# A hybrid decoder trunk on one core: for every fourth weight unit the high part comes by a GpSimd DMA instead of a ScalarE copy

## The chip, the core and the metric

The kernel runs on one core of a Trainium2 chip. What counts is the device time of one execution in microseconds (us), the median over runs. Before the change it is 2649.82 us (3 runs, 2649.51 to 2650.46).

The core has five engines that run side by side: TensorE (PE in the profile; its weight loads are PEld), VectorE (DVE), ScalarE (ACT), GpSimd (POOL) and SyncE (SP, which here only issues DMAs).

## The reference

A trunk of two layers over 256 tokens of 2048 features, in float32. Layer 0 mixes tokens by retention (8 heads), layer 1 by sliding-window attention (32 query heads, 4 key/value heads). Each layer then has a SwiGLU network of hidden width 5632 and a gated embedding.

```python
for i in range(DEPTH):
    h = rmsnorm(x, norm_mix[i])
    if i % N_MIXERS == 0:
        x = x + retention_mixer(h, ret_w_in[j], ret_gn[j], ret_w_out[j])
    else:
        x = x + swa_mixer(h, swa_w_in[j], swa_sinks[j], swa_w_out[j])
    x = x + swiglu(rmsnorm(x, norm_ffn[i]), ffn_w_in[i], ffn_w_out[i])
    gate = jax.nn.sigmoid(rmsnorm(x, norm_ple[i]) @ ple_w_gate[i])
    x = x + gate * (p[i] @ ple_w_proj[i])
return rmsnorm(x, norm_final)
```

Nearly all of the work is in the products of activations with weights. The weights, about 0.49 GB, are read from memory once.

## The kernel before

**Split products.** A float32 product is made of float32r parts: an activation and a weight are each split into a high part (hi, the value rounded to float32r) and a low part (lo, the value less hi). Each product is three matmuls: hi by hi, lo weight by hi activation, hi weight by lo activation (lines 159 to 161).

**Units and chunks.** A chunk is 512 output columns for all 256 tokens, summed up in two PSUM tiles. It is made of units: 256 rows of a weight by 512 columns, 512 KB that lie in memory in one piece, 4 KB for each of 128 partitions. A unit gives 2 row blocks x 2 token tiles x 3 = 12 matmuls of 512 columns. There are 928 units in one list over six stages: retention (units 0 to 255; a head's q and k, v, and g are 8 units each), network 0 (to 519), embedding 0 (to 555), attention (to 627), network 1 (to 891), embedding 1 (to 927).

**Buffers and order.** `run` walks the list. In step i it loads unit i + LOADS (5) into a raw buffer by one SP DMA (`load`), splits unit i + AHEAD (3) in `split_weights` (ACT copies raw to hi on line 208, DVE subtracts on line 209), and multiplies unit i. Behind a chunk's last unit its `done` takes the sums out of PSUM. Then comes one step of the side work: pieces of the heads' own work, transposes by DVE (line 233, four for each step), and the splits of the next activation. There are 5 raw, 4 hi and 4 lo buffers of 4 KB a partition. A raw buffer is free when the unit's subtraction is done, a hi or lo buffer when the unit's matmuls are done.

Each engine works off its instructions in a fixed order. This order comes from a planner that goes by the order of the code, but lets an instruction that it holds to be ready go ahead of one that is not.

**The start.** The first norm's activation (xT) comes transposed from memory in eight pieces, which pass through the raw buffers too (`load_x`, line 744): the first three between the loads of units 0, 1 and 2, the others in the side work of steps 0 to 4. ACT and DVE put a piece in place (lines 211 and 212). In the same steps x itself is loaded in four pieces.

**GpSimd** does little: two fills at the start, and 24 powers (`pow`) of a few columns, of which the retention's rs (line 360) come two for each head, after DVE's statistics of a head's output.

Of the kernel before, what the change touches and what calls it, by code (L numbers as in the profile page):

```python
# [18 lines left out]
P = 128  # L19
D = 2048  # L20
S = 256
# [17 lines left out]
STEP = 4  # L39
LOADS = 5  # L40
AHEAD = 3


class Lhs:
    """A transposed activation, split exactly into two float32r parts."""

# [8 lines left out]
class Chunk:  # L55
    """512 output columns for all tokens, accumulated over the whole contraction, in pieces of
    a token tile and some of the columns."""

# [6 lines left out]
class Unit:  # L65
    """KU blocks of 128 rows of a weight, in one chunk's columns."""

    def __init__(self, chunk, src, kts, lhs):
        self.chunk, self.src, self.kts, self.lhs = chunk, src, kts, lhs
        self.w = None  # L70


class Stage:
    """A part of the trunk with tiles of its own, from its first unit to its last."""

# [3 lines left out]
    def linear(self, w, block, lhs, done, units=None, chunk=None):  # L79
        """One chunk: block of 512 columns of a weight laid out by `_units`."""  # L80
        ch = chunk or Chunk(self, done)
        for u in units if units is not None else range(w.shape[1]):
            self.units.append(Unit(ch, w[block, u], range(KU * u, KU * u + KU), lhs))
            ch.left += 1
# [3 lines left out]
def tile_trunk(ctx, tc, ins, out):  # L88
    nc = tc.nc
    pool = ctx.enter_context(tc.tile_pool(name="persist", bufs=1))  # L90
    wraw = ctx.enter_context(tc.tile_pool(name="wraw", bufs=5))
    whi = ctx.enter_context(tc.tile_pool(name="whi", bufs=4))
    wlo = ctx.enter_context(tc.tile_pool(name="wlo", bufs=4))
# [13 lines left out]

    # ---------------------------------------------------------------- streams
    side = deque()
# [15 lines left out]
    def load(u, pieces=1):  # L125
        raw = wraw.tile([P, KU, NW], F32, name="raw")
        n = KU // pieces
        u.parts = [slice(j, j + n) for j in range(0, KU, n)]
        for part in u.parts:
            nc.sync.dma_start(raw[:, part, :], u.src[:, part, :])  # L130
        u.w = raw

    def split_weights(u):
        raw = u.w
        hi = whi.tile([P, KU, NW], F32R, name="hi")
        lo = wlo.tile([P, KU, NW], F32R, name="lo")
        for part in u.parts:
            split(hi[:, part, :], lo[:, part, :], raw[:, part, :])
        u.w = (hi, lo)

    def multiply(u, which, left):
        """The unit's products for some pieces of its chunk; `left` of the chunk's units are
        still to come."""
        ch = u.chunk
        need(u.lhs, u.kts)
        if ch.acc is None:
            ch.acc = []
            for n, (_, cols) in enumerate(ch.pieces):
                bank, name = (ps_acc, "acc") if n < NT else (ps_at, "at")
                ch.acc.append(bank.tile([P, NW], F32, name=name)[:, : cols.stop - cols.start])  # L150
        hi, lo = u.w
        for j, k in enumerate(u.kts):
            first = not ch.begun and j == 0
            last = left == 0 and j == KU - 1
            for n in which:
                t, cols = ch.pieces[n]
                sl = slice(t * P, (t + 1) * P)
                xh, xl = u.lhs.hi[:, k, sl], u.lhs.lo[:, k, sl]
                nc.tensor.matmul(ch.acc[n], xh, hi[:, j, cols], start=first, stop=False)  # L159
                nc.tensor.matmul(ch.acc[n], xh, lo[:, j, cols], start=False, stop=False)  # L160
                nc.tensor.matmul(ch.acc[n], xl, hi[:, j, cols], start=False, stop=last)  # L161

    def run(stages, begin):
        """All units in order, their weights AHEAD units ahead; between them, steps of side work.
        The products of the units that end the last chunk go piece by piece of its output."""
        units = [(st, u) for st in stages for u in st.units]
        for n, (_, u) in enumerate(units[:LOADS]):
            if n < AHEAD:
                next(begin)
            load(u, 1 if n else KU)  # L170
            if n < AHEAD:
                split_weights(u)
# [31 lines left out]

    # ------------------------------------------------------------ small pieces
    def split(hi, lo, src, scale=None):
# [9 lines left out]
    def transpose_pair(srcs):  # L216
        """Two [128, 128] blocks of both token tiles -> a PSUM tile [128, 2, S]."""
        tr = ps_tr.tile([P, 2, S], F32, name="tr")
        for j, pair in enumerate(srcs):
            for t in range(NT):  # L220
                nc.tensor.transpose(tr[:, j, t * P : (t + 1) * P], pair[t], ident)
        return tr

    def transposes(dst, src):
        """Steps that transpose src [128, NT, 512] into dst [128, 4, S], by blocks of 32 x 32."""
        n = P // SQ
# [10 lines left out]
    def blocks(src, i):  # L237
        """Blocks 2i and 2i + 1 of 128 columns of both token tiles."""
        return [[src(t)[:, b * P : (b + 1) * P] for t in range(NT)] for b in (2 * i, 2 * i + 1)]

    class Norm:
        """Sums of squares of the residual's chunks, and the transposed residual times the gain.
        The scale by token, inv, is applied behind the product with the weights."""

# [22 lines left out]
        def places(self, c, src):  # L267
            """Steps that put a chunk's four transposed blocks in place."""
            for j in range(4):
                if j % 2 == 0:  # L270
                    yield
                self.place(4 * c + j, src[:, j, :])
# [5 lines left out]
    def residual(stage, norm, c):  # L278
        """A chunk of an output projection onto the residual, then the next norm's part."""

# [14 lines left out]

    # --------------------------------------------------------------- retention
    def retention(norm, next_norm, w_in, w_out):
# [97 lines left out]

    # ---------------------------------------------------- sliding-window attention
    def swa(norm, next_norm, w_in, w_out):
# [36 lines left out]
        def q_done_of(j):  # L434
            def q_done(acc):
# [12 lines left out]
                def scores(i):  # L448
                    """Of heads 2i and 2i + 1: the numerators and denominators' parts."""
                    ats = [ps_at.tile([P, 3 * P], F32, name="at") for _ in range(2)]  # L450
# [97 lines left out]
        for j in range(SKV):  # L548
            stage.linear(w_in, j, norm.lhs, q_done_of(j))
        # The first chunks' last units wait for the last group of heads.  # L550
        n = KD // KU
# [7 lines left out]

    # --------------------------------------------------------------------- FFN  # L560
    def ffn(layer, norm, next_norm):
# [57 lines left out]

    # --------------------------------------------------------------------- PLE  # L620
    def ple(layer, norm, next_norm, final):
# [12 lines left out]
        def pair(c):  # L634
# [3 lines left out]
            def gate_done(acc):  # L638
# [7 lines left out]
                def later():  # L646
                    # The last reads of the old operand are queued: its place is free.
                    for b, xt in enumerate(st["xt"]):
                        yield from next_norm.places(b, xt)
# [34 lines left out]
            def gate_last(acc, t, cols):  # L684
                """A piece of the last chunk; with a token tile's last one, its rows go out."""
                fin, rest, row = st["fin"], st["rest"], xs[:, t, :]
# [37 lines left out]

    # ------------------------------------------------------------------- trunk
    norms = [Norm(w, layer) for layer in range(DEPTH) for w in range(3)] + [Norm(None, 0)]
# [14 lines left out]
    def load_x():  # L741
        """The first norm's operand comes transposed, in step with the first chunk's weights."""
        for b in range(KD // KU):
# [19 lines left out]
def _constants():  # L763
    """Tables that follow from the shapes alone."""
    h = np.arange(RH, dtype=np.float64)
# [14 lines left out]
def _units(w):  # L780
    """[K, N] -> [N / 512, K / 256, 128, 2, 512]: each unit in one piece, by partitions."""
    k, n = w.shape
    return w.reshape(k // (KU * P), KU, P, n // NW, NW).transpose(3, 0, 2, 1, 4)


def _heads(w):
    """The retention's columns by heads: q and k, v, g."""
    q, k, v, g = np.split(w, [RH * RK, 2 * RH * RK, 2 * RH * RK + RH * RV], axis=1)
    parts = [a.reshape(D, RH, -1) for a in (q, k, v, g)]
    return np.concatenate(parts, axis=2).reshape(D, -1)  # L790
# [44 lines left out]
```

## Time and profile before

| what | value |
|---|---|
| median of the runs | 2649.82 us |
| span of the profiled execution, first to last instruction | 2647.9 us |
| its granted TensorE clock, mean | 0.999 |
| PE busy | 2629.2 us, 99% |
| DVE busy | 1817.2 us, 69% |
| ACT busy | 1223.7 us, 46% |
| POOL busy | 14.6 us, 1% |
| read from memory | 493.63 MB, 187 GB/s over the span |

The profiled execution's own time is its span and what lies around it. The record holds the span alone; the median of the runs is 1.9 us above it. Busy time of PE is modelled for pipelined matmuls, so that it is not a measure of how near PE is to its peak.

### The profile page before, as it was taken

What the parts mean: (1) busy time and instruction counts of PE and PEld (TensorE: products, weight loads), DVE (VectorE), ACT (ScalarE), POOL (GpSimd) and SP (SyncE); (2) the same over time, 40 slices, a digit from 0 to 9 for tenths busy, and PEclk for the clock granted to TensorE, in tenths of its full rate; (3) what the DMA queues carried; (4) which work ended last, traced back from release to release, by engine and by line L of the source; (5) the groups of instructions that cost most, each with busy time, mean ns of one, the idle gap of its engine ahead of it and who ended that gap; (6) DMA issues with size and microseconds to landing.
All of it is one profiled execution on the core that took longest, in us unless ns stands there. A gap on an engine that the chain in (4) does not pass through costs nothing.

```text
span 2647.9 us, 31279 instructions
## 1 busy us (share of the span) xinstructions
PE 2629.2 (99%) x11632; PEld 2142.7 (81%) x11632; DVE 1817.2 (69%) x2567; ACT 1223.7 (46%) x1527; POOL 14.6 (1%) x30
## 2 busy tenths in 40 slices
PE   8999999999999999999999999999999999999998
PEld 6888888888888888888888887777888888888887
DVE  6777777766666667676555786888757575755565
ACT  6444444444444444444444555555444444444444
POOL 0000000000000000000000000000000000000000
PEclk9999999999999999999999999999999999999999
DMA  8555555565566565656655655346666666555564
GB/s 277 185 185 186 185 186 183 181 190 184 194 192 193 191 197 190 198 186 197 190 187 187 190 193 169 121 135 202 189 198 189 197 194 194 192 188 187 189 207 144
DMA packets 140506, 497.79 MB, mean 188 GB/s; under 512 B 15809, under 2 KB 19009, under 8 KB 140225
## 3 DMA queue, kind: packets, MB, share of 16 engines
q1 hardware_dynamic: 140064, 495.73, 58.5%
q8 instruction: 91, 1.49, 0.2%
q14 instruction: 63, 0.51, 0.1%
q10 hardware_dynamic: 288, 0.07, 0.0%
HBM read 493.63 MB, written 2.10 MB: 187 GB/s over the span
## 4 chain that ended last, share of the span: by engine, by line
PE 95%; DVE 3%; issue 1%; DMA 1%; ACT 0%; SPq 0%; ACTq 0%; POOLq 0%; POOL 0%; DVEq 0%
PE acc L159 31%; PE acc L161 31%; PE acc L160 31%; DVE lo L209 1%; DVE xt L233 1%; PE at L454 1%; PE tr L506 0%; PE at L532 0%; DMA raw<-in_ret_w_in 0%; PE at L323 0%; DVE xTl L212 0%; DVE qkT L233 0%; DMA xs<-in_x 0%; PE at L350 0%; PE at L352 0%
## 5 line engine op out<-in xcount | busy, mean ns | idle before, releaser
L209 DVE TENSOR_TENSOR lo<-raw,hi 128x1024 fp32r<-128x1024 f32 (+1 forms) x929 | 1131.8, 1221 | 720.2 <-ACT hi L208 712.8
L208 ACT ACTIVATE hi<-raw 128x1024 fp32r<-128x1024 f32 (+1 forms) x929 | 982.0, 1058 | 1210.9 <-PE acc L161 1117.4
L159 PE MATMUL acc<-hi,xTh 128*128 128x512 f32 x2592 | 1011.0, 390 | 6.6 <-ACT hi L208 5.4
L161 PE MATMUL acc<-hi,xTl 128*128 128x512 f32 x2592 | 1008.0, 389 | 0.8 <-DVE xTl L212 0.6
L160 PE MATMUL acc<-lo,xTh 128*128 128x512 f32 x2592 | 1008.7, 389 | 0.0
L159 PEld LDWEIGHTS acc<-hi,xTh 128*128 128x128 f32 x2592 | 487.3, 188 | 111.6 <-ACT hi L208 5.6
L161 PEld LDWEIGHTS acc<-hi,xTl 128*128 128x128 f32 x2592 | 487.0, 188 | 103.6 <-DVE xTl L212 2.5
L160 PEld LDWEIGHTS acc<-lo,xTh 128*128 128x128 f32 x2592 | 487.3, 188 | 100.5 <-issue 0.7
L161 PE MATMUL acc<-hi,hTl 128*128 128x512 f32 x704 | 278.4, 396 | 0.0
L160 PE MATMUL acc<-lo,hTh 128*128 128x512 f32 x704 | 278.4, 395 | 0.0
L159 PE MATMUL acc<-hi,hTh 128*128 128x512 f32 x704 | 278.4, 395 | 0.0
L233 DVE STREAM_TRANSPOSE xt<-h 32x256 f32<-32x256 f32 x352 | 153.6, 436 | 6.8
L161 PEld LDWEIGHTS acc<-hi,hTl 128*128 128x128 f32 x704 | 132.2, 188 | 32.1
L160 PEld LDWEIGHTS acc<-lo,hTh 128*128 128x128 f32 x704 | 132.2, 188 | 32.1
L159 PEld LDWEIGHTS acc<-hi,hTh 128*128 128x128 f32 x704 | 132.2, 188 | 31.9
L233 DVE STREAM_TRANSPOSE xt<-xs 32x256 f32<-32x256 f32 x320 | 139.5, 436 | 6.0
L161 PE MATMUL acc<-hi,yTl 128*128 128x512 f32 x256 | 101.2, 396 | 0.0
L160 PE MATMUL acc<-lo,yTh 128*128 128x512 f32 x256 | 101.2, 395 | 0.0
L159 PE MATMUL acc<-hi,yTh 128*128 128x512 f32 x256 | 101.2, 395 | 0.0
L233 DVE STREAM_TRANSPOSE qkT<-qk 32x256 f32<-32x256 f32 x128 | 55.8, 436 | 10.2 <-ACT qk L315 8.1
L211 ACT ACTIVATE xTh<-xt,gains 128x256 fp32r<-128x256 f32 x80 | 35.8, 499 | 56.0 <-DVE xt L233 51.6
L159 PEld LDWEIGHTS acc<-hi,yTh 128*128 128x128 f32 x256 | 48.1, 188 | 11.7
(124 smaller groups left out, 1178.2 us busy)
## 6 DMA issues: line engine op xcount, KB each, us to landing
raw<-in_ffn_w_in SPq DMA_DIRECT2D x352, 512.0 KB, 4.2
raw<-in_ret_w_in SPq DMA_DIRECT2D x191, 512.0 KB, 3.6
raw<-in_ffn_w_out SPq DMA_DIRECT2D x176, 512.0 KB, 4.0
raw<-in_ret_w_out SPq DMA_DIRECT2D x64, 512.0 KB, 4.0
raw<-in_ple_w_gate SPq DMA_DIRECT2D x64, 512.0 KB, 3.8
raw<-in_swa_w_in SPq DMA_DIRECT2D x40, 512.0 KB, 3.7
raw<-in_swa_w_out SPq DMA_DIRECT2D x32, 512.0 KB, 3.7
raw<-in_ple_w_proj SPq DMA_DIRECT2D x8, 512.0 KB, 4.0
```

Source lines behind the costliest of these rows:

```text
L159: nc.tensor.matmul(ch.acc[n], xh, hi[:, j, cols], start=first, stop=False)
L160: nc.tensor.matmul(ch.acc[n], xh, lo[:, j, cols], start=False, stop=False)
L161: nc.tensor.matmul(ch.acc[n], xl, hi[:, j, cols], start=False, stop=last)
L208: nc.scalar.activation(hi, src, AF.Copy)
L209: nc.vector.tensor_tensor(lo, src, hi.bitcast(F32), op=ALU.subtract)
L211: nc.scalar.activation(hi, src, AF.Copy, scale=scale)
L233: nc.vector.transpose(dst[b * SQ : (b + 1) * SQ, :, :, a, :], src[a * SQ : (a + 1) * SQ, :, :, b, :])
L454: nc.tensor.matmul(ats[e][:, 0:P] if b == 0 else ats[e][:, P : 3 * P], qT[sl, i, b * P : (b + 1) * P], kT[sl, j, 0 : (b + 1) * P], start=True,
```

## The change

For every fourth unit, from the sixth unit on (5, 9, 13, ... 925, in all 231), hi is not copied by ACT: when the unit is loaded, a GpSimd DMA reads the same 512 KB from memory a second time and writes them as float32r into a hi buffer. DVE then subtracts over the whole unit as before. hi has five buffers and raw four, so that the sum of the buffers stays, and loads run four units ahead in place of five. The diff also empties some comments and descriptions, left out here.

```diff
-LOADS = 5
+LOADS = 4
...
-        self.w = None
+        self.w = self.hi = None
+        self.cast = False
...
-    wraw = ctx.enter_context(tc.tile_pool(name="wraw", bufs=5))
-    whi = ctx.enter_context(tc.tile_pool(name="whi", bufs=4))
+    wraw = ctx.enter_context(tc.tile_pool(name="wraw", bufs=4))
+    whi = ctx.enter_context(tc.tile_pool(name="whi", bufs=5))
...
         u.w = raw
+        if u.cast:
+
+            u.hi = whi.tile([P, KU, NW], F32R, name="hi")
+            nc.gpsimd.dma_start(u.hi, u.src)
...
-        hi = whi.tile([P, KU, NW], F32R, name="hi")
+        hi = u.hi or whi.tile([P, KU, NW], F32R, name="hi")
         lo = wlo.tile([P, KU, NW], F32R, name="lo")
-        for part in u.parts:
-            split(hi[:, part, :], lo[:, part, :], raw[:, part, :])
+        if u.cast:
+            nc.vector.tensor_tensor(lo, raw, hi.bitcast(F32), op=ALU.subtract)
+        else:
+            for part in u.parts:
+                split(hi[:, part, :], lo[:, part, :], raw[:, part, :])
...
         units = [(st, u) for st in stages for u in st.units]
+        for n, (_, u) in enumerate(units[LOADS:]):
+            u.cast = n % 4 == 1
```

## Rows read from the trace of the kernel before

**Rows 1.** The page's first part: busy us, share of the span, instructions.
```profile
PE 2629.2 (99%) x11632; PEld 2142.7 (81%) x11632; DVE 1817.2 (69%) x2567; ACT 1223.7 (46%) x1527; POOL 14.6 (1%) x30
```
**Rows 2.** Waits of PE: engine, line, what ended them: us, times, longest.
```profile
PE acc L159 <- ACT hi L208: 5.4, 1, 5.4
PE at L323 <- DVE qkT L233: 1.5, 1, 1.5
PE acc L159 <- ACT xTh L211: 1.2, 2, 0.9
PE acc L160 <- DVE lo L209: 1.1, 1, 1.1
```
**Rows 3.** Groups by line: count, busy us, mean ns, idle us before.
```profile
L209 DVE TENSOR_TENSOR lo<-raw,hi 128x1024 fp32r<-128x1024 f32 (+1 forms) x929 | 1131.8, 1221 | 720.2 <-ACT hi L208 712.8
L159 PE MATMUL acc<-hi,xTh 128*128 128x512 f32 x2592 | 1011.0, 390 | 6.6 <-ACT hi L208 5.4 <-ACT xTh L211 1.2
...
L208 ACT ACTIVATE hi<-raw 128x1024 fp32r<-128x1024 f32 (+1 forms) x929 | 982.0, 1058 | 1210.9 <-PE acc L161 1117.4 <-issue 64.3 <-ACT hi L208 10.3
```
**Rows 4.** Timeline of ACT around 1000 us: start us, us, instruction, idle before.
```profile
1000.42 1.06 ACT L208 ACTIVATE hi<-raw 128x1024 fp32r<-128x1024 f32 x1 [1.66 <-PE acc L161]
1003.14 1.06 ACT L208 ACTIVATE hi<-raw 128x1024 fp32r<-128x1024 f32 x1 [1.66 <-PE acc L161]
```
**Rows 5.** Windows: length, busy us by engine, granted clock, DMA share, GB/s.
```profile
0.00:38.00 38.00, 31.29 (x120) 23.97 (x121) 22.70 (x35) 28.44 (x50) 1.41 (x7) 1.00 0.93 332
38.00:556.00 518.00, 516.47 (x2292) 427.56 (x2292) 389.58 (x565) 235.14 (x261) 8.64 (x16) 1.00 0.58 185
1757.00:1832.00 75.00, 73.52 (x315) 58.79 (x316) 68.22 (x115) 37.74 (x59) 0.69 (x1) 1.00 0.54 171
```
**Rows 6.** DMA queues (packets, MB, share) and issues (count, KB, us to landing).
```profile
q1 hardware_dynamic: 140064, 495.73, 58.5%
...
raw<-in_ffn_w_in SPq DMA_DIRECT2D x352, 512.0 KB, 4.2
...
xs<-in_x SPq DMA_DIRECT2D x4, 512.0 KB, 5.9
```
**Rows 7.** Timeline of SP's queue at the start.
```profile
3.21 0.43 SPq L745 DMA_DIRECT2D raw<-in_xT  x1
5.31 6.26 SPq L130 DMA_DIRECT2D raw<-in_ret_w_in  x4
```
**Rows 8.** The chain that ended last, at the start: start us, us, what.
```profile
8.26 4.37 DMA raw<-in_ret_w_in
12.65 1.07 ACT hi L208
13.75 1.24 DVE lo L209
```
**Rows 9.** Timeline of PE: the first matmul of unit 2, the 25th in all.
```profile
13.76 0.39 PE L159 MATMUL acc<-hi,xTh 128*128 128x512 f32 x1
```
**Rows 10.** Timelines of DVE and PE in the retention's third head.
```profile
176.80 1.23 DVE L209 TENSOR_TENSOR lo<-raw,hi 128x1024 fp32r<-128x1024 f32 x1
...
181.57 2.25 DVE L233 STREAM_TRANSPOSE qkT<-qk 32x256 f32<-32x256 f32 x5
...
185.50 0.60 PE L323 MATMUL at<-qkT 128*128 128x256 f32 x2
```
**Rows 11.** Timeline of POOL in the same head.
```profile
200.88 0.54 POOL L360 TENSOR_TENSOR rs<-ve,mhalf 128x1 f32<-128x1 f32 x1 [64.30 <-DVE ve L358]
```
**Rows 12.** Timeline of DVE in the attention's output projection.
```profile
1780.83 7.17 DVE L233 STREAM_TRANSPOSE xt<-xs 32x256 f32<-32x256 f32 x16
1788.03 1.23 DVE L209 TENSOR_TENSOR lo<-raw,hi 128x1024 fp32r<-128x1024 f32 x1
```

## The prediction

> **What bounds the kernel now.** I read the page's busy times first, then the waits of TensorE, then the groups by line, and last timelines of the places where a wait could arise. TensorE (PE) is busy 99% of the span; VectorE (DVE) 69% and ScalarE (ACT) 46% [rows 1]. Such a share alone proves little, since matmuls are pipelined; the waits do: in 2647.9 us PE waits 9.2 us in four entries, 5.4 of it for the very first weights [rows 2]. One weight unit (256 rows by 512 columns) is 12 matmuls, and the ScalarE copies that follow the units' ends come 2.72 us apart [rows 4], so PE issues one matmul each 0.227 us although each lasts 0.39 us [rows 3]. There are 928 units; 928 x 2.72 = 2524 us, the rest is the heads' own PE work. ACT has nothing to do most of the time: before its copies it sits idle 1211 us, 1117 us of that because a hi buffer is still being read by PE [rows 3]. So a copy taken from ACT takes nothing from the end. The windows show three kinds of stretch [rows 5]: the first 38 us, where PE is idle 6.7 us and the DMA engines are 93% busy at 332 GB/s; the steady stretches, with DMA at 58%; and 1757 to 1832, where DVE is busy 68.2 of 75 us and PE idle 1.5.
>
> **The ScalarE copy that goes.** Of the units from the sixth on every fourth (5, 9, ... 925: 231 units) loses its ACT copy, 231 x 1.06 = 245 us of ACT [rows 3]. It lies beside PE work and nothing else waits for ACT's time: 0 us. The DVE subtraction stays, 1.22 us for each unit, in one instruction as before.
>
> **Five hi buffers, asked for in another order.** The DMA's hi is asked for with the load, four units ahead, a copied hi three units ahead. So the order of the buffers is 5, 4, 6, 7, 9, 8, 10, 11. If the five go round strictly, unit 8 takes the buffer of unit 5 and waits for unit 5's products, where before it waited for unit 4's; the others get theirs one to two units earlier. If a buffer goes to the next who asks when it is freed, unit 8 waits for unit 4 as before. The bounds are therefore 0 and one unit, 2.72 us, on every fourth copy. In steady stretches this is covered: copy and subtraction take 1.06 + 1.22 = 2.3 us; before they had three units, 8.2 us, now two, 5.4 us, and 3.1 us are left. Queued behind that copy on ACT are the next copies and the chunk's evacuation, behind that subtraction on DVE the transposes; PE needs those late only in two places. In the retention, DVE works through 16 transposes and three subtractions with hardly a gap, the last transposes end at 183.82 and PE uses them at 185.50, behind unit 60 [rows 10]: 1.7 us to spare. The subtraction that starts there at 176.80 is unit 60's own, of the late kind: unit 57 ends three units before 185.5, at 177.3, the copy some 1.1 later, so it would start at 178.5, 1.7 us late, which uses up what was to spare. I allow 0.1 a head, for eight heads 0 to 0.8 us, and take 0.4. The order on DVE in these rows is not that of the code (five transposes between two subtractions, where the code yields after four), so the planner may also fill the hole with transposes. In 1757 to 1832 DVE is the bound already: 16 transposes run for 7.17 us and the subtraction behind them makes PE wait 1.1 us [rows 2, 12]. A subtraction whose hi comes late there costs only if DVE has nothing else ready: 0, bounded by six such units x 2.72 = 16 us.
>
> **Four raw buffers and loads.** A raw buffer now comes back after four units, 10.9 us, not five, 13.6. Landing 4.2 [rows 6], copy and subtraction 2.3: 6.5 us, so 4.4 us are left for queues, 7.1 before. In steady stretches 0. At the start it is not: the activation's pieces xT go through the same buffers. The third xT piece went out at 3.21 and unit 2's weights at 5.31, when the first xT piece had been placed [rows 7]; with four buffers the former waits for that placing, and unit 2's weights for unit 0's subtraction, which releases the next issue at 8.26 in the trace of before. That row's own landing, copy and subtraction end at 14.99 [rows 8], and the second matmul of unit 2 stood at 13.76 + 0.23 [rows 9]: 1.0 us late.
>
> **The 231 DMAs from GpSimd (POOL).** They add 231 x 0.524 = 121 MB to the 495.7 MB of SP's queue [rows 6]. In steady stretches a unit's load keeps the DMA engines 58% busy [rows 5]; a fifth load in four units makes 72% at equal cost, and they would be full at 2.9 times the cost per byte (58 + 14.5c = 100). The trace has no GpSimd DMA and no converting one. Nearest rows: the same 512 KB from SP land in 4.2 us, in the crowded start 5.9 [rows 6]; I take 5. By the buffer order such a DMA may start when the unit six before is done and its subtraction must start 5 x 2.72 - 1.22 = 12.4 us later, so 0 us while it lands within 12.4. On POOL it can stand behind a `pow` that waits for DVE (rs, two for each of eight heads): the one of 200.88 [rows 11], asked for after unit 64, stands in front of unit 69's DMA if code order rules. It is over at 201.4, about when unit 65 ends; three units and six matmuls of the head, 8.2 + 1.4 = 9.5 us, still lie before unit 69, less 1.2 for the subtraction 8.3: over the 5. At the start nothing holds unit 5's DMA: its buffer is new, so it goes out among the first loads, where the DMA engines are full: 0.524 MB at 332 GB/s is 1.6 us for everything behind it. Lower bound 0 (it lands where a gap was), upper bound 4.7 us (units 5, 9 and 13 all pay). PE waited there for the xT pieces, 0.9 and 0.3 [rows 2], so a delay of them passes to PE. I take one DMA, 1.6, plus the 1.0 of the raw buffers, less the 0.3 wait that absorbs some: 2.3 us.
>
> **A rule that speaks against it.** The subtraction handles 1024 elements a partition in 1.22 us [rows 3]; a run of 16 transposes and one subtraction, 7.17 + 1.23 = 8.4 us, has no gap [rows 12]; the sum above takes 0 for both. The Trainium skill ("SBUF — State Buffer", Who interferes with whom) holds that VectorE and GpSimd share a pair of ports under an exclusive lock, which a VectorE instruction in a two-port mode takes, and that a GpSimd DMA is then starved of descriptors; tensor_tensor, it says, has no such mode. By the rule the subtraction would cost nothing either, while the transposes, of which it says nothing, could; the sum would then be rival C's. No row of before shows a GpSimd DMA beside either.
>
> **Sum.** The profiled execution has a span of 2647.9 us; the three runs' median, 2649.8, is 1.9 above it, which I carry along. 2649.8 + 2.3 (start) + 0.4 (retention) = 2652.5 us, 0.1% more. What a measurement can tell from no change is 0.2%, 5.3 us: from 2655.1 on it is slower.
>
> **Rivals.**
> A, the start costs more: all three early DMAs and the raw buffers are paid, 4.7 + 1.0 = 5.7, with retention 2655.9: just slower. For it: 93% DMA share. Against: weights there have slack, only xT pieces have none. 17%.
> B, the new DMA is slow: at 13 us each of the 231 units costs 0.6, 139 us, 2791. It decides from 12.4 us, or from 2.9 times the cost per byte. For it: a converting transfer is not in the trace; against: the margin is three times the nearest row. 5%.
> C, the new DMA can start only when DVE pauses: in steady stretches DVE pauses in every unit, but in 1757 to 1832 a run of 8.4 us and a landing of 5 make 13.4, 1.0 us over, for six units 6 us: 2658. It decides from runs of 7.4 us. The page named above has a rule of this kind. 3%.
> D, late copies stall DVE where it is the bound (1757 to 1832 and the attention before it): half of the 16 us is 8, giving 2660 with the start's 2.3. It decides from 2.6 us beyond the start's cost. For: DVE is 91% busy there; against: the planner's reordering, and that DVE has transposes to put in the hole. 12%.
> E, nothing happens: the early DMA falls into gaps, 2649.8. 8%.
> F, faster: outside its first 5.4 us PE waits under 4.4, so even all of it gained is below 5.3. 2%.
> That ACT is not relieved at all could be only if the copies stayed; the diff drops them.
>
> **Numbers.** Forecast 53%, E 8%: same 61%. A, B, C, D: 17 + 5 + 3 + 12, slower 37%. F, faster, 2%. The range 2648 to 2666 holds the forecast, A, C, E and most of D; out are B and the upper part of D, up to 2668, and what of F goes below. The forecast's own range is 2650 to 2655.
>
> **What the profile will show.** Right if PE's waits stay near 10 us, nearly all before 40 us, the ACT copies number 698 in place of 929, DMA share in steady stretches is about 72%, the GpSimd DMA lands in 4 to 6 us, and matmuls still follow at 0.227 us. Wrong if DVE's subtractions wait for the DMA in each fourth unit (B or C), if PE waits for lo between 1580 and 1832 (D), or if matmuls themselves get slower beside the extra traffic, of which no row here tells anything.

## The result: 6.1 us slower, lost in the first 63 us

The changed kernel takes 2656.61 us (median of 8 runs, 2655.31 to 2659.35), the kernel before 2650.51 us beside it (8 runs, 2649.51 to 2651.57). The ratio is 1.0025 with an interval of 1.0015 to 1.0034: slower by about 6.1 us, 4.0 to 9.0 by the interval. The forecast was 2652.5. What came is rival A, "the start costs more", with 2655.9.

The profiled execution has a span of 2656.1 us, an own time of 2658.28, so it is one of the longer of the eight. Its page answers to [rows 1, 6] like this (busy times by engine, then the DMA queues: packets, MB, share):

```profile
PE 2631.4 (99%) x11632; PEld 2144.0 (81%) x11632; DVE 1808.8 (68%) x2567; ACT 988.6 (37%) x1296; POOL 139.6 (5%) x261
...
q1 hardware_dynamic: 140064, 495.73, 56.9%
q0 software_dynamic: 33264, 121.13, 15.3%
```

ScalarE has shed 235 us and 231 instructions, GpSimd has gained 125 us and 231, and PE has the same count and practically the same busy time. The 121 MB are there, on a queue of their own. In share of the DMA engines per byte this queue costs 1.10 times what SP's costs (15.3 / 121.13 against 56.9 / 495.73).

PE's waits after (us, times, longest), against [rows 2]:

```profile
PE acc L167 <- ACT hi L218: 7.3, 2, 5.7
PE acc L167 <- ACT xTh L221: 3.1, 3, 2.4
PE at L333 <- DVE qkT L243: 2.2, 1, 2.2
PE acc L168 <- DVE lo L219: 1.7, 2, 1.2
PE acc L169 <- DVE xTl L222: 0.8, 2, 0.4
```

15.1 us in five entries. [rows 2] has four, 9.2 us; a fifth of that trace, 0.6 us for xTl, is missing there and in the prediction, so that 9.8 is the like sum. The waits have grown for ACT's hi (5.4 before), for the transposed activation xTh (1.2 before) and for the first head's qkT (1.5 before): all things of the start. The wait of 1.2 us for lo is the one that the kernel before has too (1.1), in the attention's output projection. (Lines are ten further down than before: 167 to 169 are the matmuls, 218 and 219 the copy and the subtraction, 143 the subtraction of a unit with a DMA of its own, 136 that DMA.)

The windows of [rows 5] after (length; busy us of PE, PEld, DVE, ACT, POOL; granted clock; DMA share; GB/s):

```profile
0.00:38.00 38.00, 27.69 (x97) 20.16 (x98) 18.29 (x30) 22.22 (x43) 2.13 (x9) 0.96 0.87 295
38.00:556.00 518.00, 515.67 (x2281) 426.65 (x2280) 386.49 (x564) 192.11 (x219) 33.92 (x61) 1.00 0.72 232
1757.00:1832.00 75.00, 73.80 (x320) 57.89 (x319) 64.40 (x107) 31.93 (x51) 3.95 (x7) 1.00 0.64 208
1765.00:1840.00 75.00, 73.09 (x313) 58.32 (x313) 68.35 (x114) 31.34 (x52) 3.99 (x7) 1.00 0.65 215
```

In the first 38 us PE is busy 3.6 us less and the clock is below 1.00. In the long stretch the DMA share has gone from 0.58 to 0.72 and PE has lost only 0.8 us (the stretch holds the qkT wait at 54 us). The last stretch, where DVE was the bound, lies some 8 us later now, so the window 1765 to 1840 is the one to set beside 1757 to 1832 of before: PE is busy 73.09 us there, before 73.52, and DVE 68.35, before 68.22.

The plainest reading is to lay the same matmul of the two traces side by side. The first matmul of unit 15 and that of unit 550, before:

```profile
54.80 0.39 PE L159 MATMUL acc<-hi,xTh 128*128 128x512 f32 x1
...
1548.55 0.39 PE L159 MATMUL acc<-hi,xTh 128*128 128x512 f32 x1
```

and after:

```profile
62.81 0.39 PE L167 MATMUL acc<-hi,xTh 128*128 128x512 f32 x1
...
1556.56 0.39 PE L167 MATMUL acc<-hi,xTh 128*128 128x512 f32 x1
```

1493.75 us lie between them in both. The changed kernel is 8.01 us behind at unit 15 and 8.01 us behind at unit 550, 535 units and 134 GpSimd DMAs later; at unit 920 it is 7.98. How far the changed kernel lies behind (the *lag*, from here on) is taken in this way at other units, where every twelfth of the matmuls into acc counts as the start of a unit:

| unit | 0 | 2 | 3 | 4 | 7 | 11 | 13 | 15 | 550 | 920 |
|---|---|---|---|---|---|---|---|---|---|---|
| us behind | 0.3 | 1.2 | 3.2 | 4.4 | 5.2 | 5.8 | 6.9 | 8.0 | 8.0 | 8.0 |

(At unit 7 the two traces have their matmuls in a different order; its own first matmul is 5.6 us behind.) From unit 15 to 550 the lag stands still. In the attention behind that it moves, to 9.2 and down to 7.0, and is 7.9 at unit 640. It moves there in the experiments too, so single traces say little below 1 to 2 us from there on.

Where the first 4.4 us come from stands in SP's queue (start, us, issue) after, against [rows 7]:

```profile
2.71 0.47 SPq L131 DMA_DIRECT2D raw<-in_ret_w_in  x1
5.69 0.38 SPq L755 DMA_DIRECT2D raw<-in_xT  x1
9.46 1.28 SPq L131 DMA_DIRECT2D raw<-in_ret_w_in  x2
10.79 0.43 SPq L763 DMA_DIRECT2D xs<-in_x  x1
12.57 0.33 SPq L131 DMA_DIRECT2D raw<-in_ret_w_in  x1
13.36 0.38 SPq L755 DMA_DIRECT2D raw<-in_xT  x1
```

The third xT piece waits from 3.2 to 5.69 for a raw buffer. Unit 2's weights go out at 9.46, not 5.31. A first piece of x (512 KB that nobody on PE's path needs yet; before, at 15.43) is put ahead in the meantime by the planner, and the fourth xT piece goes out behind it. ACT places that piece only here:

```profile
20.19 0.89 ACT L221 ACTIVATE xTh<-raw,gains 128x256 fp32r<-128x256 f32 x2
```

and PE, which waits 2.4 us for it, starts unit 3 at 20.73, before at 17.56. At the same time GpSimd's queue shows unit 5's DMA among the first loads, and then nothing for 23.5 us:

```profile
1.44 0.70 POOL L136 DMA_DIRECT2D hi<-in_ret_w_in  x1
25.65 0.53 POOL L136 DMA_DIRECT2D hi<-in_ret_w_in  x1 [23.51 <-PE acc L169]
```

It lands at 7.88. Beside it the second half of unit 0's weights lands at 8.06 (6.86 before), the second xT piece at 8.94 (7.55) and unit 1 at 10.20 (8.88): each 1.2 to 1.4 us later.

Two more pieces of the lag in this execution come from the clock. Windows of the changed kernel around them (columns as above):

```profile
15.00:21.00 6.00, 3.50 (x14) 2.25 (x13) 2.37 (x3) 4.17 (x8) 0.00 (x0) 1.00 0.93 338
21.00:24.40 3.40, 3.40 (x9) 2.62 (x9) 3.26 (x6) 2.23 (x7) 0.00 (x0) 0.50 0.86 288
...
51.00:55.00 4.00, 1.81 (x8) 1.22 (x8) 3.87 (x7) 1.67 (x2) 0.00 (x0) 1.00 0.77 253
55.10:58.50 3.40, 3.40 (x12) 2.83 (x11) 2.64 (x5) 0.52 (x1) 0.00 (x0) 0.51 1.02 348
```

After the xTh wait, in which PE was busy 3.50 of 6 us, the granted clock is 0.50 (the level of 1.2 GHz) for 3.4 us; after the qkT wait, with PE busy 1.81 of 4 us, the same once more. The lag grows by 1.23 us from unit 3 to unit 4 and by 1.12 from unit 13 to unit 14, in these stretches. Before the change the clock shows no fall from its rise at 11.0 us to the last 7 us of the span.

### The profile page after: what moved, and what is told of

Read it like the earlier page. It is cut to its first block, busy times and chain, and to the rows that moved or that the text cites. A ratio compares the mean times of both kernels' runs of the same rounds, so it can differ in the third digit from the quotient of the medians.

```text
span 2656.1 us, 31788 instructions
## 1 busy us (share of the span) xinstructions
PE 2631.4 (99%) x11632; PEld 2144.0 (81%) x11632; DVE 1808.8 (68%) x2567; ACT 988.6 (37%) x1296; POOL 139.6 (5%) x261
## 3 DMA queue, kind: packets, MB, share of 16 engines
q1 hardware_dynamic: 140064, 495.73, 56.9%
q0 software_dynamic: 33264, 121.13, 15.3%
## 4 chain that ended last, share of the span: by engine, by line
PE 94%; DVE 3%; DMA 1%; issue 1%; ACT 0%; SPq 0%; ACTq 0%; POOLq 0%; POOL 0%; DVEq 0%
PE acc L167 30%; PE acc L169 30%; PE acc L168 30%; DVE xt L243 1%; DVE lo L219 1%; DMA raw<-in_ret_w_in 1%; PE at L464 1%; PE at L542 0%; PE tr L516 0%; PE at L333 0%; DMA xs<-in_x 0%; DMA raw<-in_xT 0%; DVE qkT L243 0%; PE at L360 0%; PE at L362 0%
## 5 line engine op out<-in xcount | busy, mean ns | idle before, releaser
L218 ACT ACTIVATE hi<-raw 128x1024 fp32r<-128x1024 f32 (+1 forms) x698 | 738.2, 1059 | 1316.4 <-PE acc L169 1179.3
L219 DVE TENSOR_TENSOR lo<-raw,hi 128x1024 fp32r<-128x1024 f32 (+1 forms) x698 | 851.7, 1221 | 534.1 <-ACT hi L218 301.4
L143 DVE TENSOR_TENSOR lo<-raw,hi 128x1024 fp32r<-128x1024 f32 x231 | 282.6, 1223 | 206.7 <-DMA hi<-in_ffn_w_in 62.7
L136 POOL DMA_DIRECT2D hi<-in_ffn_w_in x88 | 47.0, 534 | 902.3 <-PE acc L169 529.7
```

The costliest lines, as they stand in the source:

```text
L136: nc.gpsimd.dma_start(u.hi, u.src)
L143: nc.vector.tensor_tensor(lo, raw, hi.bitcast(F32), op=ALU.subtract)
L218: nc.scalar.activation(hi, src, AF.Copy)
L219: nc.vector.tensor_tensor(lo, src, hi.bitcast(F32), op=ALU.subtract)
```

## The experiments

The question is where the start loses 6 us, of which the forecast had 2.3: to four raw buffers, to the GpSimd DMAs of units 5, 9 and 13, or to both together. The edits are shown against the changed kernel.

### Four combinations of buffers and early DMAs

Late DMAs only, with the changed buffers:

```diff
-        for n, (_, u) in enumerate(units[LOADS:]):
-            u.cast = n % 4 == 1
+        for n, (_, u) in enumerate(units[4:]):
+            u.cast = n % 4 == 1 and n > 12
```

> The changed kernel, but the GpSimd DMAs of units 5, 9 and 13 are left out (ACT copies those units), so that the first is that of unit 17; four raw and five hi buffers stay. The changed kernel's lag behind the kernel before is 8.0 us at unit 15 and the same at unit 550. Theory 1, the start is slower both by the raw buffers and by the early DMAs: 2653 to 2654 us, a lag of 2 to 4 us at unit 15. Rival 1, the raw buffers alone: 2656.6, lag 8. Rival 2, the early DMAs alone: 2650.5, lag below 1.

The changed buffers with no GpSimd DMA at all:

```diff
-        for n, (_, u) in enumerate(units[LOADS:]):
-            u.cast = n % 4 == 1
```

> No GpSimd DMA at all: every unit's hi is copied by ACT; four raw buffers, loads four ahead, five hi buffers. If all DMAs after the start cost nothing, this is e1_late_casts within 0.5 us: theory 1 gives 2653 to 2654, rival 1 2656.6, rival 2 2650.5. If the 228 later DMAs cost something, it is below e1_late_casts by that.

All 231 DMAs with the buffers of before:

```diff
-LOADS = 4
+LOADS = 5
...
-    wraw = ctx.enter_context(tc.tile_pool(name="wraw", bufs=4))
-    whi = ctx.enter_context(tc.tile_pool(name="whi", bufs=5))
+    wraw = ctx.enter_context(tc.tile_pool(name="wraw", bufs=5))
+    whi = ctx.enter_context(tc.tile_pool(name="whi", bufs=4))
...
-        for n, (_, u) in enumerate(units[LOADS:]):
+        for n, (_, u) in enumerate(units[4:]):
```

> All 231 GpSimd DMAs, but with the buffers of before (five raw, four hi, loads five ahead); the order of SP's first loads is again that of before. A DMA's buffer is then free three units ahead of its use, 8.2 us less 1.2 for the subtraction, where the landing in the changed kernel was 5.4 to 6.3 us. Theory 1: the early DMAs' part of the lag stays, 2 to 4 us at unit 15, 2653 to 2654. Rival 1 (raw buffers alone): 2650.5. Rival 2 (early DMAs alone): lag 8, 2656.6. If the narrower window is too narrow, waits of DVE for the DMA reach PE in the steady stretches and the lag grows from unit to unit.

The same without the first three, so that 228 of the 231 DMAs are left and no early one (on top of the edit above):

```diff
-            u.cast = n % 4 == 1
+            u.cast = n % 4 == 1 and n > 12
```

> Five raw and four hi buffers, loads five ahead, GpSimd DMAs from unit 17 on (228). Theory 1 and both rivals: the start is that of the kernel before, lag below 0.5 us at unit 15, 2650.5 at the end if the later DMAs cost nothing; no gain below the kernel before, since PE waits for nothing that ACT does.

All four ran beside the kernel before, whose median there was 2650.45 us (33 runs; 11 of each of the four); the change has its own 2650.51 beside it:

| kernel | raw/hi buffers | DMAs | median us | against before | ratio and interval | lag at unit 15 |
|---|---|---|---|---|---|---|
| e4 | 5/4 | 228, none early | 2650.50 | +0.05 | 1.0000, 0.9992 to 1.0009 | 0.4 |
| e3 | 5/4 | all 231 | 2653.03 | +2.6 | 1.0008, 1.0000 to 1.0017 | 2.1 |
| e2 | 4/5 | none | 2653.50 | +3.05 | 1.0009, 1.0000 to 1.0018 | 2.6 |
| e1 | 4/5 | 228, none early | 2653.80 | +3.35 | 1.0014, 1.0005 to 1.0022 | 2.8 |
| the change | 4/5 | all 231 | 2656.61 | +6.1 | 1.0025, 1.0015 to 1.0034 | 8.0 |

Two readings. First, the 228 later GpSimd DMAs cost nothing that these runs can tell: e4 stands at 1.0000 beside before, and e1 at 0.3 us from e2, which has none. Nor do the copies taken from ACT bring anything. (In e4's traced execution PE's wait for lo in the attention's output projection is 2.2 us, before 1.1, and the lag goes from 0.4 at unit 550 to 1.1 at unit 920; the median of 11 runs doesn't show it.) Second, both the buffers and the three early DMAs cost: 3.05 to 3.35 us for the one, 2.6 for the other, where the change has 6.1. The intervals of e2 and e3 reach down to 1.0000, and those of neighbours in the table overlap; of e3 and e4 the runs themselves hardly do, 2651.48 to 2653.57 against 2649.22 to 2651.75.

That the two costs simply add up is a reading of medians, and it gets weaker when the clock is taken into account. Each execution comes with its mean granted clock. In the traces of this case 0.999 goes with no fall before the last 10 us of the span (before, e2, e5, e8, e9), 0.998 or 0.997 with one or two falls (the change has two; e1 has one, from 19.6 us, behind a wait for xTh as in the change; e3 and e4 have one each, near 1790 us). Medians against before, sorted by it:

| kernel | executions at 0.999 | us against before | executions below | us against before |
|---|---|---|---|---|
| e4 | 6 | -0.1 | 5 | +0.5 |
| e3 | 4 | +1.8 | 7 | +2.8 |
| e2 | 4 | +1.3 | 7 | +3.5 |
| e1 | 6 | +2.9 | 5 | +4.1 |
| the change | 4 | +6.0 | 4 | +7.1 |

So the change loses its 6 us without any fall of the clock, while most of e2's executions seem to have had one. Without falls, buffers (1.3 or 2.9) and early DMAs (1.8) make 3.1 to 4.7, less than 6.0. Whether the two make each other worse is not shown; the numbers in each group are small.

PE's waits in e2 name what is late with the buffers alone:

```profile
PE acc L167 <- ACT hi L216: 5.6, 1, 5.6
PE at L331 <- DVE qkT L241: 2.6, 1, 2.6
PE acc L167 <- ACT xTh L219: 2.0, 3, 0.8
```

The wait for xTh has grown by 0.8, that for qkT by 1.1: the latter is the first head's transposes, which DVE does beside the same late subtractions (at 48.63 us, four of them, where before the last four ran at 46.05).

### Which of the early DMAs

```diff
-            u.cast = n % 4 == 1
+            u.cast = n % 4 == 1 and n > 1
```

> The changed kernel without the GpSimd DMA of unit 5 alone, which is issued at 1.44 us among the first loads; units 9, 13 and on keep theirs. The changed kernel is at 2656.6, without the DMAs of 5, 9 and 13 it was 2653.8. If the DMA in front of the first loads is what costs: 2654, as without all three, lag 2.8 at unit 15. If the three share it evenly: 2655.7. If it is those of 9 and 13, issued at 25.7 and 39.6: 2656.6.

2655.08 us (11 runs) beside 2650.26 of before: +4.8, ratio 1.0019 (1.0010 to 1.0027). That is 1.3 us less than the change with all three, between the first expectation and the second. By the medians unit 5's DMA costs 1.3 us, and those of units 9 and 13 the 1.5 us that are left to e1's 3.35. But the intervals of the change, of this run and of e1 overlap each other, and the executions at a clock of 0.999 say it otherwise: e5 is at +3.2 (4 of its 11 runs), so that unit 5's DMA would cost 2.8 and the other two 0.2. How the loss divides among the three is open. In e5's profiled execution the clock doesn't fall, and the lag at unit 15 is 3.9.

### More DMAs, to find where they begin to cost

Every second unit from unit 17 on, and every unit from 17 on:

```diff
-            u.cast = n % 4 == 1
+            u.cast = n % 2 == 1 and n > 12
```

> From unit 17 on every second unit's hi comes by a GpSimd DMA (455 in place of 228); the start is that of the run without early DMAs, 2653.8. In the changed kernel 121 MB on the GpSimd queue took 15.3% of the DMA engines over the span and SP's loads 56.9%, so here 57 + 30 = 87%. Theory: below 100%, PE keeps its step of 2.72 us a unit, 2653 to 2656, and ACT's busy time falls by another 240 us without any use. Rival, late landings: at this share the DMAs land later than the 9 to 12 us that the buffers leave, and the lag grows from unit to unit, over 2665.

```diff
-            u.cast = n % 4 == 1
+            u.cast = n > 12
```

> From unit 17 on every unit's hi comes by a GpSimd DMA (911). Shares add to 57 + 61 = 118% of the DMA engines at the span of before, so the DMA engines would be the bound: 2650 x 1.18 = 3127 us if a transfer costs what it costs now; 991 MB at the 332 GB/s of the first 38 us would be 2985 us, at 400 GB/s 2650 and PE would still be the bound. Expected 2950 to 3150, PE waiting for hi and lo in every unit; the rival that the engines have more left than the share says gives under 2750.

With every second unit 2665.94 us (4 runs), ratio 1.0059 (1.0046 to 1.0073): 15.7 us more, some 12 more than the buffers alone, where I had expected nothing. The DMA engines are 84% busy from 100 to 500 us and the networks' long stretch loses nothing (the lag is 11.7 at unit 256 and at unit 550). The loss lies in the retention, where the lag grows by some 1 us with each head, and later in the attention. PE's waits say for what:

```profile
PE at L361 <- DVE vl L222: 6.0, 5, 2.1
```

vl is the low part of a head's values, made by DVE between subtractions. The rival's number was right and its mechanism wasn't: the 456 DMAs (the expectation counts 455) land in 5.4 us (median), each at least 3.5 us before its unit's products. The waits point to DVE's order in the heads and not to the DMA engines; why vl comes late was not tried by itself.

With every unit 2733.51 us (2 runs, 2725.72 and 2741.3), ratio 1.0314 (1.0287 to 1.0340). Two of its windows, the first in the retention and the second in network 0, and its queues:

```profile
100.00:500.00 400.00, 383.38 (x1644) 314.57 (x1643) 281.29 (x413) 34.73 (x62) 74.04 (x139) 0.97 0.98 345
760.00:1500.00 740.00, 736.29 (x3195) 597.99 (x3194) 465.75 (x578) 40.56 (x77) 141.73 (x267) 1.00 1.05 379
```

```profile
q0 software_dynamic: 131184, 477.68, 50.4%
q1 hardware_dynamic: 140064, 495.73, 49.4%
...
hi<-in_ffn_w_in POOLq DMA_DIRECT2D x352, 512.0 KB, 6.7
```

The DMA engines are full here, but that alone does not bound the kernel: where they are busiest, in the network (379 GB/s), PE is still busy 736 of 740 us. The loss lies in the retention, where the lag is 42.6 us by unit 256, and in the attention, where it grows from 51 at unit 550 to 78 at unit 625. The largest of PE's waits is for the heads' transposes:

```profile
PE at L333 <- DVE qkT L243: 21.9, 8, 3.5
```

The clock also falls ten times, for 51 us in all. How much of the loss is due to which has not been separated. The rival's "under 2750" was right, the theory that put it at 2950 or more wrong: the two queues carried 973 MB in a span of 2739 us, 355 GB/s, more than the 332 of the crowded start [rows 5], and the shares per byte of the two are 1.06 to 1.

### Is it the order of the x loads?

Each load of x waits for the xT piece before it (a one-column GpSimd copy into x's place stands ahead of it), so that it can't be put ahead:

```diff
         for b in range(KD // KU):
+            prev = x0 if b else None
             x0 = wraw.tile([P, KU, NW], F32, name="raw")[:, :, 0:S]
...
+                nc.gpsimd.tensor_copy(xs[:, 0, c * NW : c * NW + 1], prev[:, 0, 0:1])
                 nc.sync.dma_start(
```

> The changed kernel with one thing more: each 512 KB piece of x waits until the xT piece before it has landed (a one-column copy on GpSimd ahead of each load), so that the first x piece no longer goes out at 10.8 us in front of three weight units and the fourth xT piece. If that early x piece is part of the lag: the fourth xT piece lands some 1.5 us earlier than 19.8, the lag at unit 4 falls from 4.4 to about 3, 2655. If not, 2656.6 and the same lag.

2658.75 us (6 runs), ratio 1.0031 (1.0019 to 1.0043): not better. The early part does what it should: the fourth xT piece lands at 18.09 and not 19.79 (a load of 128 KB for the decay table now goes ahead in place of x), the lag at unit 4 is 1.5 and not 4.4, and the clock doesn't fall. But at unit 7 the lag is 5.5, at unit 15 6.8, at the end 8.1: a load that is held back holds back what stands behind it in SP's queue, and the last xT piece lands at 34.86, in the change at 34.56, before at 29.94. So the x piece put ahead explains the place of the loss; since the edit brings delays of its own, the run doesn't show how much of the loss it explains.

### Buffers of their own for xT

The pieces of xT get two buffers of half a unit's size, and hi goes back to four to make room; raw stays at four and loads at four ahead. Without any GpSimd DMA:

```diff
-    whi = ctx.enter_context(tc.tile_pool(name="whi", bufs=5))
+    whi = ctx.enter_context(tc.tile_pool(name="whi", bufs=4))
+    wx = ctx.enter_context(tc.tile_pool(name="wx", bufs=2))
...
-        for n, (_, u) in enumerate(units[LOADS:]):
-            u.cast = n % 4 == 1
...
-            x0 = wraw.tile([P, KU, NW], F32, name="raw")[:, :, 0:S]
+            x0 = wx.tile([P, KU, S], F32, name="x0")
```

> No GpSimd DMA, four raw buffers and loads four ahead as in the change, hi back at four buffers, and the memory so freed holds two half-size buffers through which the eight xT pieces pass, so that they take no raw buffer any more. Theory S (the raw buffers cost because weight loads and xT pieces share four of them, so that a load waits for a piece to be placed and the other way round): the lag behind before at unit 15 falls from 2.6 us to under 1, the median to within 1.0 us of before. Rival L (loads four ahead are too short for the crowded start, whoever holds the buffers): lag 2 to 3 us, median 2.5 to 3.5 above before. Rival X (two buffers are too few for the pieces themselves, so xT is later still): lag above 3 and PE waits for xTh above 3 us.

and with all 231 (the same edit, the two lines with `cast` kept):

> The same with all 231 GpSimd DMAs, the ones of units 5, 9 and 13 too. If the early DMAs and the buffers add up, as the medians of the four combinations did (0, 2.6, 3.3, 6.1 us), the three early DMAs cost 2 to 3 us on top of the run without them. If the DMAs cost only where xT pieces and weights already wait for each other, they cost under 1 us on top.

e9 takes 2649.29 us (11 runs) beside 2649.66 of before, ratio 0.9998 (0.9989 to 1.0007), and the lag at unit 15 is -0.1. Theory S holds: four raw buffers and loads four ahead cost nothing once xT doesn't pass through them. All eleven executions have a granted clock of 0.999, where e2 had seven below it. SP's queue in e9:

```profile
5.55 0.33 SPq L754 DMA_DIRECT2D x<-in_xT  x1
5.92 1.79 SPq L132 DMA_DIRECT2D raw<-in_ret_w_in  x3
8.46 0.33 SPq L754 DMA_DIRECT2D x<-in_xT  x1
```

Three weight loads are out by 7.7 us, for which the changed kernel needs until 12.9, and the fourth xT piece goes at 8.46, not 13.36.

e10 missed both expectations: 2667.01 us (5 runs), ratio 1.0062 (1.0050 to 1.0075), 17.4 us above before. The start is as the first one had it, roughly: the lag at unit 15 is 1.7, 1.8 more than in e9 (2 to 3 expected). But then it grows, to 7.1 at unit 400, 9.1 at 550 and 17.1 at the end. PE's waits:

```profile
PE acc L169 <- DVE lo L220: 9.5, 11, 2.2
```

What differs from the changed kernel behind the start is the fifth hi buffer. With five, a DMA is issued 0.3 us after the unit six before it has ended, and a copied hi of every fourth unit starts as soon as the unit four before ends; with four hi and four raw, both come one unit, 2.72 us, later (3.02 us after the unit six before and 2.76 us after the unit four before, medians of units 300 to 500). The DMAs land in nearly the same time (median 5.9 us). Of the two, e4 speaks for the DMA's request as what costs: there, with four hi and five raw, that copied hi starts as late (2.76 us after the unit four before), but the DMA goes out 0.3 us after the unit six before as in the change, and nothing is lost. e3's expectation, which had the request come later with four hi, was wrong in this. So the fifth hi buffer, or a fifth raw buffer with loads five ahead, is what makes the 228 later DMAs free. The waits for lo are 9.1 of the 15.4 us that e10 loses behind unit 15 (0.4 of the row's 9.5 lie before it); where the rest lies I have not separated.

No version here beats the kernel before; e4 and e9 equal it.

## Why the prediction was nearly right, and where it failed

**What bounds the kernel.** Right. The copies 2.72 us apart have gone on as before, 1493.75 us from unit 15 to unit 550 in both traces, and the 235 us taken from ACT bought nothing, since 1316 us of its idle time lie before the copies that are left.

**The term that failed: "I take one DMA, 1.6, plus the 1.0 of the raw buffers, less the 0.3 wait that absorbs some: 2.3 us."** The place was right, the size not: the medians have 6.1, and the profiled execution 8.0. The range, 2648 to 2666, held the result. Of the parts:

- The raw buffers, forecast 1.0, cost 3.05 alone (e2) and 3.35 under late DMAs (e1), or 1.3 and 2.9 in the executions without a fall of the clock. The 1.0 was worked out for one load, unit 2's, and it was about right for that one: in e2 unit 2 is 0.5 us late, in the change its second matmul stands at 15.51, forecast 14.99. But the working stopped there. Each later xT piece and load has the same wait for a buffer, and the lag in e2 goes on to 1.4 at unit 7 and 2.6 at unit 13, where the first head's transposes are late too. e9 shows the cause as the prediction named it, the sharing of raw buffers between xT and weights: without it the same four raw buffers cost nothing.
- The early DMAs, forecast as one, 1.6, cost 2.5 together with five raw buffers (e3 against e4) and 2.8 with four (the change against e1), inside the bounds of 0 to 4.7. Unit 5's is 1.3 by the medians and 2.8 by the executions without a fall; so whether those of units 9 and 13 fell into gaps, as forecast, stays open.
- The 0.3 that PE's waits absorb wasn't there: the waits for xTh grew, from 1.2 to 3.1 us.
- Not in the sum at all: the clock, which fell twice for 3.4 us in the profiled execution, 1.23 and 1.12 us of its 8.0. No run tried it by itself, but the median doesn't need it: the four executions at 0.999 have 2656.51.
- Whether buffers and DMAs together cost more than each alone was not in the sum either, and is open.

Rival A had the right mechanism and, with 5.7 us, nearly the size; its way there was another (4.7 for all DMAs and 1.0 for the buffers, where the medians have 2.8 and 3.35), so that the near hit of its number is luck.

**The order of the hi buffers.** "0 and one unit" were the bounds; it is the lower. In steady stretches the copied hi of a unit like 8 starts 0.04 us after the unit four before has ended, so a buffer goes to the next who asks when it is freed. With it falls the 0.4 for the retention: the lag at unit 15 and at unit 550 is the same, and all eight heads' ends lie before unit 256, at the same lag.

**The DMA itself.** Taken at 5 us, it lands in 5.5 (median of 231; 5.4 for ffn_w_in, 6.3 for ret_w_in, at most 8.4), and everywhere at least 4.0 us before the products of its unit. The share of 72% came out to the digit, the byte at 1.10 times SP's. B (12.4 us) is refuted. DVE's subtraction does wait for the DMA at times, in the changed kernel (the two largest rows):

```profile
DVE lo L143 <- DMA hi<-in_ffn_w_in: 62.7, 29, 3.4
DVE lo L143 <- DMA hi<-in_ffn_w_out: 44.2, 20, 4.8
```

The prediction called such waits a sign against it; 75 of all 231 subtractions wait so, at most 4.8 us, and the lag stands still from unit 15 to 550: the sign was chosen too sharply. It is PE's wait that counts, as in e10.

**C and the rule on ports.** The stretch that C was about has this in the changed kernel, DVE's and GpSimd's timelines:

```profile
1788.26 7.18 DVE L243 STREAM_TRANSPOSE xt<-xs 32x256 f32<-32x256 f32 x16
```

```profile
1787.22 0.54 POOL L136 DMA_DIRECT2D hi<-in_swa_w_out  x1 [10.66 <-PE acc L169]
```

The DMA of 1787.22 lands after 6.4 us, at 1793.7, in the midst of the 16 transposes, which run without a gap from 1788.26 to 1795.44. It didn't wait for DVE to pause; SP's own load, issued in the same microsecond, took 6.3. Since it was issued 0.5 us before the run began, it doesn't show what happens to one that is issued during transposes; the other DMAs do. Of the 231, 30 are issued wholly beside transposes and 146 wholly beside subtractions: they keep GpSimd for 0.54 and 0.53 us and land in 5.0 and 6.5 us (medians), none in over 8.4. SP's loads issued beside them take 4.0 and 5.9, so the difference is not one of GpSimd's DMAs.

The Trainium skill's rule ("SBUF — State Buffer", Who interferes with whom) ties the lock to VectorE's two-port modes; tensor_tensor, it says, has none, but with both inputs in SBUF contends with GpSimd's reads. The trace agrees in so far as neither subtractions nor transposes hold up a GpSimd DMA in the numbers above.

**D.** In 1765 to 1840 PE is busy 73.09 us, in the window of before 73.52, and it waits once for lo, 1.2 us, where before it waited once for 1.1:

```profile
1796.76 0.49 PE L168 MATMUL acc<-lo,oTh 128*128 128x512 f32 x1 [1.20 <-DVE lo L219]
```

So D's late copies, priced at 8 us, didn't come in the change. Something of the kind shows where that wait is 2.2 us (e3, e4) and in e10, where PE waits 9.5 us for lo in all.

**The chances.** The likeliest case, same, didn't come; slower had 37%, and A's 17% hold the result. Since all that could go wrong at the start went in one direction (each bound of the early DMAs and of the raw buffers was a loss, and nothing there could gain), a value near the lower end of the bounds of the early DMAs was too bold.

## What to carry to other kernels

A kernel whose matmul engine never waits in its steady stretches can still lose where its buffers are shared with something else: look at the first loads before any steady sum, and follow a lack of buffers through all the loads that come after, not through the first alone. A transfer without a dependency goes out with the very first loads; with the buffers of before, a start some units later (e4) made it cost nothing. Whether a prefetch by a slower way is free depends on how early its buffer is asked for: one buffer fewer moved each request by 2.7 us, and e10 lost 15 us behind unit 15 with it, where the transfers themselves cost nothing (e4). And a time that moves by 1 to 2 us with the clock wants its executions sorted by clock before small terms are read from medians.

## What the runs showed of the hardware that was not expected

A GpSimd DMA of 512 KB that converts float32 to float32r keeps GpSimd for 0.54 us and lands in 5.5 us, while the same bytes by SP's queue land in 4.3 to 4.5; its share of the DMA engines per byte is only 1.10 times as large (1.06 with both queues full), and full queues carried 345 GB/s in the retention and 379 in a network, with PE busy 736 of 740 us beside it. TensorE's clock went to the 1.2 GHz level for 3.4 us after two short stretches in which PE had waited 2.2 and 2.4 us; in e2's traced execution a wait of 2.6 us for the same qkT brought no fall, so that what decides is left open here.
